# Sums of squares per token from ScalarE squares and column-tiled matmuls, in a two-block network on one core

## The chip, the core and the metric

The kernel runs on one core of a Trainium2 chip. A core has five engines with queues of their own: TensorE (PE, with a unit for loading weights, PEld), VectorE (DVE), ScalarE (ACT), GpSimd (POOL) and SyncE (SP, which here starts most transfers). Each takes its instructions in order, and semaphores hold an instruction until what it reads is written, or what it overwrites has been read. SBUF is the on-chip memory of 128 partitions; PSUM is where TensorE writes its sums, and ACT and DVE can read it. The metric is the device time of one execution, in microseconds.

## The reference

The reference is a network for 256 tokens of width 1024, in float32. A first block has a layer with a hybrid mixer and a dense feed-forward, and a layer with a Mamba-2 mixer and a mixture of eight experts. A second block has an even and an odd mixer, each with a squared-ReLU MLP, and works on the latent tokens and on a second set of 256 context tokens. In front of every mixer and feed-forward stands a normalization over the 1024 values of a token, followed by a modulation. The experts are chosen by router logits of the modulated tokens.

```python
def rmsnorm(x, w):
    y = xf * lax.rsqrt(jnp.mean(xf * xf, axis=-1, keepdims=True) + NORM_EPS)
    return y * w
def modulate(x, norm_w, shift, scale):
    return rmsnorm(x, norm_w) * (1 + scale) + shift
def moe_ffn(h, router, w_gu, w_down):
    logits = h @ router                        # 256 x 8
    top_val, top_idx = lax.top_k(logits, TOP_K)
    ...
# first block, the layer with experts
            mix = mamba2_mixer(modulate(x, ssm_norm[i], shift, scale), ...)
            x = x + gate * mix
            ffn = moe_ffn(modulate(x, moe_norm[i], shift, scale), ...)
            x = x + gate * ffn
```

So the sum of xf * xf over the 1024 values of each token is needed at each normalization.

## The kernel before

The activations are kept transposed: `x` is a tile of 128 partitions by 8 by 256, where the 1024 values of a token lie over 128 partitions and 8 slices k, and the 256 tokens are columns. `cx` is the same for the context. Weights are streamed from HBM by SP (`raw`, line 421), split by ACT into a rounded half `whi` and by DVE into the rest `wlo` (lines 426 and 429), and multiplied in three matmuls per pair (lines 446 to 448, 508 to 511, 565 to 567). Projections go to PSUM tiles `pws`, `praw`, `pm`; the output projection of a mixer or an MLP sums in `oacc` (lines 565 to 567), and then DVE adds it into `x` slice by slice (`resid`, line 891).

`square_sums` (line 598) gives the sum of squares of each token. Eight slices times two halves of the tokens make sixteen matmuls: a slice of 128 tokens is both the stationary and the moving operand, so that the 128x128 result in PSUM (`pss`) has the sums on its diagonal. DVE then multiplies each of two results with the identity and sums the rows (line 610), which gives one column of sums for each half. `rstd` scales on DVE (line 593) and takes the power -1/2 on POOL (line 595); `tok_rows` (line 631) multiplies the column by the identity on PE, which writes the factor of each token into every partition (`prb`). `norm_k` applies factor and modulation (lines 709 to 711: DVE, ACT, DVE).

There are twelve calls: at the start (`rms`, line 2553); in front of the dense feed-forward and of the Mamba mixer (`raw_mod`, line 681, where the projection runs on unnormalized data, `praw`, and the factor `rb` is applied to its result); in front of the experts (line 1564); two in the double normalization between the blocks (`two_norms`, lines 649 and 652); four for latent and context in the second block (`rms`, after each slice of the output projection has been added); one more `raw_mod` in front of the last MLP; and one at the end (line 2607).

In front of the experts the router's logits are sixteen matmuls (line 1571) with a slice of `x` as stationary operand and 8 columns of `AR` (router times modulation) as moving operand; DVE scales them by the factor of the token and adds the part of the shift (line 1574, `lg`). Ranks, lists of tokens per expert, the gathering matmuls (line 1672) and the experts' weights follow.

At the start the filters of the odd mixer are made while the first transfers run: a matmul `pfl` (line 2088), an eviction `fl` on DVE (line 2089), an absolute value on ACT (line 2091), summing matmuls `phn` with ones (line 2092), a reciprocal on DVE (line 2094), further products on DVE (lines 2101 to 2105), and the transform `pH` (line 2117). Between them PE computes the modulation `pada` (line 828): four matmuls of 128x32 by 512 columns, each into another group of 32 columns of the array.

The order of the instructions on each engine is not that of the code: a planner in the framework places each instruction where its operands are expected to be ready, so work of neighbouring steps stands between the parts of a function. `h_t` is a tag of two buffers in which `norm_k` and `square_sums` keep short-lived tiles.

## Time and profile before

| quantity | value |
| --- | --- |
| time, median of three | 2732.47 us (2728.77 to 2732.86) |
| the profiled execution | 2731.91 us, its span 2729.8 us |
| TensorE busy | 2612.9 us (96%) |
| VectorE busy | 1805.1 us (66%) |
| ScalarE busy | 1141.4 us (42%) |
| GpSimd busy | 74.1 us (3%) |
| granted clock of TensorE, mean | 0.986 of full speed |
| HBM traffic | 240 GB/s over the span |

The time of an execution is a little longer than the span, which runs from the first to the last instruction in the profile. Busy times of engines overlap. The ends of matmuls are modelled and matmuls are pipelined, so their lengths add up to more than the time that they hold PE; how long a group holds PE is read from the start of the next group. In the order of events, brackets give how long the engine sat idle before an instruction and whose end released it; a row with xN gathers N records without a break. A float32 matmul makes two records.

### The profile page before, as it was taken

To read this page: it belongs to the slowest core of one execution; us is meant where nothing else is said; L and a number is where in the kernel's file an instruction comes from. 1 tells how busy PE (TensorE), PEld (TensorE's weight loads), DVE (VectorE), ACT (ScalarE), POOL (GpSimd) and SP (SyncE) were. 2 spreads that over 40 slices of the span, in tenths; PEclk is the share of its full clock that TensorE was granted. 3 is DMA by queue.
4 is the path that set the end of the run, shared out by engine and by line. 5 is a ranking of instruction groups with operands and counts; after the bars stand their busy time and mean duration, and the time that the engine had idled before them with its cause. 6 is when DMAs were issued, how large, how long until landed. Compare 5 with 4: busy or idle time off the path is not lost. (4 is left out here: it accounts for less than half of the span.)

```text
span 2729.8 us, 42989 instructions
## 1 busy us (share of the span) xinstructions
PE 2612.9 (96%) x17432; PEld 2090.2 (77%) x17432; DVE 1805.1 (66%) x2970; ACT 1141.4 (42%) x1635; POOL 74.1 (3%) x117
## 2 busy tenths in 40 slices
PE   6999999999899999999999999989999999989999
PEld 2768999879755665566555589479889999879999
DVE  5485888887645655555545579678857548787754
ACT  3354445554644444444444432443223225313543
POOL 0100000000000000000000000000000001000000
PEclk9999999999899999999999999989999999999999
DMA  7655885543799999999999932334555303302552
GB/s 253 221 186 203 338 336 208 189 179 139 288 406 423 408 425 421 413 372 420 411 413 422 381 123 78 139 147 155 210 191 216 124 18 104 121 9 91 205 187 90
DMA packets 92780, 659.49 MB, mean 242 GB/s; under 512 B 10548, under 2 KB 10821, under 8 KB 13918
## 3 DMA queue, kind: packets, MB, share of 16 engines
q1 hardware_dynamic: 89582, 641.62, 60.1%
q0 software_dynamic: 2992, 15.04, 1.6%
q8 instruction: 139, 2.28, 0.3%
q14 instruction: 67, 0.55, 0.1%
HBM read 651.38 MB, written 4.72 MB: 240 GB/s over the span
## 5 line engine op out<-in xcount | busy, mean ns | idle before, releaser
L429 DVE TENSOR_TENSOR wlo<-wraw,whi 128x1024 fp32r<-128x1024 f32 (+1 forms) x683 | 811.3, 1217 | 337.9 <-ACT whi L426 334.3
L426 ACT ACTIVATE whi<-wraw 128x1024 fp32r<-128x1024 f32 (+1 forms) x683 | 705.2, 1054 | 719.1 <-PE oacc L566 182.0
L565 PE MATMUL oacc<-act_h,whi 128*128 128x256 f32 (+1 forms) x720 | 226.9, 316 | 0.0
L566 PE MATMUL oacc<-act_l,whi 128*128 128x256 f32 (+1 forms) x720 | 226.8, 315 | 0.0
L567 PE MATMUL oacc<-act_h,wlo 128*128 128x256 f32 (+1 forms) x720 | 226.8, 315 | 0.0
L794 DVE SCALAR_TENSOR_TENSOR macc<-wraw,srow 128x1024 f32<-128x1024 f32 x144 | 175.8, 1221 | 7.0 <-DMA wraw<-in_ada_dram 2.7
L567 PEld LDWEIGHTS oacc<-act_h,wlo 128*128 128x128 f32 x720 | 135.7, 188 | 10.1
L565 PEld LDWEIGHTS oacc<-act_h,whi 128*128 128x128 f32 x720 | 135.6, 189 | 10.0
L566 PEld LDWEIGHTS oacc<-act_l,whi 128*128 128x128 f32 x720 | 135.6, 188 | 10.0
L509 PE MATMUL pm<-h_lo,whi 128*128 128x256 f32 x512 | 132.8, 280 | 0.0
L508 PE MATMUL pm<-h_hi,whi 128*128 128x256 f32 x512 | 132.2, 277 | 0.0
L429 DVE TENSOR_TENSOR eal<-pat,eah 128x512 fp32r<-128x512 f32 x28 | 19.3, 691 | 167.0 <-ACT eah L426 167.0
L508 PE MATMUL pws<-h_hi,whi 128*128 128x256 f32 x416 | 112.1, 282 | 4.8 <-DVE xg L644 4.8
L1755 PE MATMUL pu<-wraw,gq 128*64 128x512 f32 x448 | 113.4, 595 | 0.0
L509 PE MATMUL pws<-h_lo,whi 128*128 128x256 f32 x416 | 111.4, 282 | 0.0
L1760 ACT ACTIVATE ea<-pg 128x512 f32<-128x512 f32 x42 | 25.1, 597 | 203.9 <-PE pg L1755 162.8
L447 PE MATMUL pyl<-wlo,eah 128*128 128x512 f32 x224 | 90.5, 404 | 18.6 <-DVE wlo L429 17.5
L511 PE MATMUL pm<-h_hi,wlo 128*128 128x256 f32 x512 | 106.9, 279 | 0.0
L446 PE MATMUL pws<-h_hi,whi 128*128 128x256 f32 x352 | 103.5, 294 | 0.0
L1761 DVE TENSOR_TENSOR ea<-ea,pu 128x512 f32<-128x512 f32 x42 | 28.9, 687 | 112.3 <-PE pu L1755 79.7
L1755 PE MATMUL pg<-wraw,gq 128*64 128x512 f32 x448 | 101.4, 596 | 0.0
L448 PE MATMUL pws<-h_hi,wlo 128*128 128x256 f32 x352 | 101.1, 287 | 0.0
(788 smaller groups left out, 6411.0 us busy)
## 6 DMA issues: line engine op xcount, KB each, us to landing
wraw<-in_moe_gu_dram SPq DMA_DIRECT2D x224, 1024.0 KB, 10.0
wraw<-in_moe_down_dram SPq DMA_DIRECT2D x112, 1024.0 KB, 9.7
wraw<-in_mlp_dram SPq DMA_DIRECT2D x64, 1024.0 KB, 4.8
wraw<-in_ada_dram SPq DMA_DIRECT2D x48, 1024.0 KB, 4.8
wraw<-in_dense_gu_dram SPq DMA_DIRECT2D x22, 1024.0 KB, 5.9
wraw<-in_hyb_mod_dram SPq DMA_DIRECT2D x12, 1024.0 KB, 6.8
wraw<-in_dense_mod_dram SPq DMA_DIRECT2D x12, 1024.0 KB, 4.8
wraw<-in_ssm_xbc_dram SPq DMA_DIRECT2D x12, 1024.0 KB, 4.8
```

Of the source, the lines that this page charges most:

```text
L426: self.nc.scalar.activation(hi, src, AF.Copy)
L429: self.nc.vector.tensor_tensor(lo, src, hi, op=OP.subtract)
L446: mm(out, l[0], r[0], start=start, stop=False)
L448: mm(out, l[1], r[0], start=False, stop=stop)
L508: mm(p[:, i], hi[:, k], hs[i][0][:, k], start=st, stop=False, skip_group_check=True)
L509: mm(p[:, i], hi[:, k], hs[i][1][:, k], start=False, stop=False, skip_group_check=True)
L511: mm(p[:, i], lo[:, k], hs[i][0][:, k], start=False, stop=k == 7, skip_group_check=True)
L565: mm(p, wh, h, start=start, stop=False, skip_group_check=True)
L566: mm(p, wh, l, start=False, stop=False, skip_group_check=True)
L567: mm(p, wl, h, start=False, stop=stop, skip_group_check=True)
L794: nc.vector.scalar_tensor_tensor(junk, r[:, j], 1.0, s, op0=OP.mult, op1=OP.mult, accum_out=t[:, f:f + 1])
L1755: mm(pg[gu][q], g[2][:, i, q], w[:, k], start=i == 0, stop=i == 7, skip_group_check=True)
```

## The change

`square_sums` is written anew. ACT squares two slices at a time into a tile of the tag `h_t` (128x512, four instructions). Eight matmuls with a stationary operand of ones, 128x32, run over 256 columns each and write 32 partitions of `pss`; slice k goes to column group k modulo 4, so that two slices are summed in each group. ACT copies the 128x256 result to SBUF, and two matmuls of one column with 1/32 as moving operand sum over the 128 partitions (each sum stands 32 times in its group), one for each half of the tokens. The result stays in PSUM, and line 593 reads it there. The sums of the router's logits are formed in the same way: `AR` is padded with zeros from 8 to 32 columns by a memset on POOL and is the stationary operand, ACT copies the four groups, and two matmuls with `four` (the sum of four pieces of the identity, from three adds on DVE) add them.

```diff
--- before.py
+++ after.py
@@ -359,6 +359,8 @@
         self.mhalf = self.cst.tile([128, 8], F32, name="mhalf")
         nc.gpsimd.memset(self.mhalf, -0.5)
         self.ident = self.k("ident")
+        self.one32 = self.cst.tile([128, 1], F32, name="one32")
+        nc.vector.memset(self.one32, 1.0 / 32)
 
     def c(self, name, i=0, n=None):
         o, w = self.at["cols"][name]
@@ -597,18 +599,22 @@
 
     def square_sums(self, x, ps=None):
 
+
         nc = self.nc
-        pss = (ps or self.ps)("pss", (128, 2, 128))
-        for k in range(8):
-            for tt in range(2):
-                c = slice(tt * 128, tt * 128 + 128)
-                nc.tensor.matmul(pss[:, tt], x[:, k, c], x[:, k, c], start=k == 0 and tt == 0, stop=k == 7,
-                                 skip_group_check=True)
-        ss = self.sm.tile([128, 2], F32, name="ss")
-        junk = self.hp.tile([128, 2, 128], F32, name="rj", tag="h_t", bufs=2)
+        pss = (ps or self.ps)("pss")
+        for k2 in range(4):
+            sq = self.hp.tile([128, 2, 256], F32, name="sqk", tag="h_t", bufs=2)
+            nc.scalar.activation(sq, x[:, 2 * k2:2 * k2 + 2], AF.Square)
+            for j in range(2):
+                k = k2 * 2 + j
+                q = slice(k % 4 * 32, k % 4 * 32 + 32)
+                nc.tensor.matmul(pss[q, :256], self.ones[:, :32], sq[:, j], start=k < 4, stop=k >= 4, skip_group_check=True)
+        part = self.hp.tile([128, 256], F32, name="sqp", tag="h_t", bufs=2)
+        nc.scalar.activation(part, pss[:, :256], AF.Copy)
+        ss = pss[:, 256:258]
         for tt in range(2):
-            nc.vector.scalar_tensor_tensor(junk[:, tt], pss[:, tt], 1.0, self.ident, op0=OP.mult, op1=OP.mult,
-                                           accum_out=ss[:, tt:tt + 1])
+            nc.tensor.matmul(ss[:, tt:tt + 1], part[:, tt * 128:(tt + 1) * 128], self.one32, start=True, stop=True,
+                             skip_group_check=True)
         return ss
 
     def col_sums(self, p, sq, start=True, stop=True):
@@ -1531,8 +1537,9 @@
 
     nc = S.nc
     R = S.c("router").rearrange("p (k e) -> p k e", e=8)
-    AR = S.cst.tile([128, 8, 8], F32, name="AR")
-    nc.vector.tensor_tensor(AR, R, S.mod(key, "A")[:, :, None].to_broadcast([128, 8, 8]), op=OP.mult)
+    AR = S.cst.tile([128, 8, 32], F32, name="AR")
+    nc.gpsimd.memset(AR, 0.0)
+    nc.vector.tensor_tensor(AR[:, :, :8], R, S.mod(key, "A")[:, :, None].to_broadcast([128, 8, 8]), op=OP.mult)
     p = S.ps("psr", (128, 8))
     s = S.mod(key, "S")
     for k in range(8):
@@ -1554,6 +1561,10 @@
         wk = st.enter_context(tc.tile_pool(reuse_waits="tile", name="moew", bufs=2))
         iota = mp.tile([128, 128], F32, name="iota")
         nc.gpsimd.iota(iota, pattern=[[1, 128]], base=0, channel_multiplier=0, allow_small_or_imprecise_dtypes=True)
+        four = mp.tile([128, 8], F32, name="four")
+        nc.vector.tensor_tensor(four, S.ident[:, 0:8], S.ident[:, 32:40], op=OP.add)
+        for q in (64, 96):
+            nc.vector.tensor_tensor(four, four, S.ident[:, q:q + 8], op=OP.add)
         st.enter_context(S.extra(raw=4, big=2))
         xr = S.rings["r"][2]
         ohp = st.enter_context(tc.tile_pool(reuse_waits="tile", name="moeh", bufs=1))
@@ -1565,10 +1576,15 @@
         r = mp.tile([128, 2], F32, name="rtok")
         nc.vector.tensor_copy(r, S.rstd(ss, 1024))
 
-        pl = S.ps("plog", (128, 2, 8))
+        pq = S.ps("plog", (128, 512))
+        for k in range(8):
+            q = slice(k % 4 * 32, k % 4 * 32 + 32)
+            mm(pq[q, :256], AR[:, k], x[:, k], start=k < 4, stop=k >= 4, skip_group_check=True)
+        lq = wk.tile([128, 256], F32, name="lq", tag="ea")
+        nc.scalar.activation(lq, pq[:, :256], AF.Copy)
+        pl = pq[:, 256:272].rearrange("p (t e) -> p t e", t=2)
         for tt in range(2):
-            for k in range(8):
-                mm(pl[:, tt], x[:, k, tt * 128:(tt + 1) * 128], AR[:, k], start=k == 0, stop=k == 7)
+            mm(pl[:, tt], lq[:, tt * 128:(tt + 1) * 128], four, start=True, stop=True, skip_group_check=True)
         lg = mp.tile([128, 2, 8], F32, name="lg")
         for tt in range(2):
             nc.vector.scalar_tensor_tensor(lg[:, tt], pl[:, tt], r[:, tt:tt + 1], SR, op0=OP.mult, op1=OP.add)
```

The planner gives other orders. The first place is DVE's queue at the start, up to the second reciprocal `finv`, and the rows begin two instructions behind the first reciprocal in before and just behind it in after. An `fl` from `pfl` is an eviction of the filter; lines 2089, 2094 and 2101 to 2105 of before are 2105, 2110 and 2117 to 2121 of after.

```order
L2103 TENSOR_TENSOR fl<-g_372,finv 128x512
L2104 TENSOR_TENSOR fl<-fl,finv 128x512
L2101 SCALAR_TENSOR_TENSOR g_377<-fl,k_hy 128x512
L2105 TENSOR_TENSOR fl<-fl,hskip 1x512
L2102 TENSOR_TENSOR fl<-fl 128x512
L2089 TENSOR_TENSOR fl<-pfl,k_hy_93 128x512 x2
L2103 TENSOR_TENSOR fl<-g_377,finv 128x512
L2104 TENSOR_TENSOR fl<-fl,finv 128x512
L2089 TENSOR_TENSOR fl<-pfl,k_hy_93 128x512
L2101 SCALAR_TENSOR_TENSOR g_383<-fl,k_hy 128x512
L2102 TENSOR_TENSOR fl<-fl 128x512
L2094 RECIPROCAL finv<-phn 128x512
```

And in the changed kernel:

```order
L2105 TENSOR_TENSOR fl<-pfl,k_hy_95 128x512 x2
L2119 TENSOR_TENSOR fl<-g_374,finv 128x512
L2120 TENSOR_TENSOR fl<-fl,finv 128x512
L2105 TENSOR_TENSOR fl<-pfl,k_hy_95 128x512
L2117 SCALAR_TENSOR_TENSOR g_379<-fl,k_hy 128x512
L2121 TENSOR_TENSOR fl<-fl,hskip 1x512
L2118 TENSOR_TENSOR fl<-fl 128x512
L2119 TENSOR_TENSOR fl<-g_379,finv 128x512
L2110 RECIPROCAL finv<-phn 128x512
```

Between the two reciprocals stand four evictions in before (the first of them is the row right behind the first reciprocal, not shown) and three in the changed kernel, because ahead of the first reciprocal stand five of them instead of four. Three products (2104, 2101 and 2102 in the lines of before) have moved from the front of the second reciprocal to behind it.

The second place is ACT's queue after the first MLP's context part (near 1866 us): `whi` is the split of a weight slice, `h_hi` the modulation, whose `Sc` is that of the context and `Sl` that of the latent tokens.

```order
L426 ACTIVATE whi<-wraw 128x1024
L710 ACTIVATE h_hi<-h_t,mod_01Sc 128x256 x2
L426 ACTIVATE whi<-wraw 128x1024
L710 ACTIVATE h_hi<-h_t,mod_01Sl 128x256 x8
L426 ACTIVATE whi<-wraw 128x1024
```

And in the changed kernel:

```order
L716 ACTIVATE h_hi<-h_t,mod_01Sc 128x256 x2
L428 ACTIVATE whi<-wraw 128x1024
L716 ACTIVATE h_hi<-h_t,mod_01Sc 128x256
L607 ACTIVATE sqk<-x 128x512 x4
L613 ACTIVATE sqp<-pss 128x256
L716 ACTIVATE h_hi<-h_t,mod_01Sl 128x256 x8
```

The four squares and the copy of the sums stand between the last weight split and the modulation of the latent tokens, behind that split.

The third place is PE's queue at the context call near 2219 us, inside the output projection of the latent tokens (`oacc`).

```order
L566 MATMUL oacc<-act_l,whi 128x256
L567 MATMUL oacc<-act_h,wlo 128x256
L605 MATMUL pss<-cx 128x128 x16
L565 MATMUL oacc<-act_h,whi 128x256
L566 MATMUL oacc<-act_l,whi 128x256
L567 MATMUL oacc<-act_h,wlo 128x256
```

And in the changed kernel:

```order
L569 MATMUL oacc<-act_h,wlo 128x256
L611 MATMUL pss<-sqk,ones 32x256 x4
L567 MATMUL oacc<-act_h,whi 128x256
L568 MATMUL oacc<-act_l,whi 128x256
L569 MATMUL oacc<-act_h,wlo 128x256
L567 MATMUL oacc<-act_h,whi 128x256
L568 MATMUL oacc<-act_l,whi 128x256
L569 MATMUL oacc<-act_h,wlo 128x256
L611 MATMUL pss<-sqk,ones 32x256 x2
L567 MATMUL oacc<-act_h,whi 128x256
L611 MATMUL pss<-sqk,ones 32x256 x2
L568 MATMUL oacc<-act_l,whi 128x256
```

The sixteen matmuls in one piece are replaced by eight tile matmuls in three pieces, with output matmuls between them.

## Rows read from the trace of the kernel before

**Rows 1.** The page: the span, and busy time of each engine.

```profile
span 2729.8 us, 42989 instructions
...
PE 2612.9 (96%) x17432; PEld 2090.2 (77%) x17432; DVE 1805.1 (66%) x2970; ACT 1141.4 (42%) x1635; POOL 74.1 (3%) x117
```

**Rows 2.** Stretches: window, length, busy PE, PEld, DVE, ACT, POOL, clock, DMA, GB/s.

```profile
75.00:246.00 171.00, 168.46 (x1117) 130.51 (x1116) 98.66 (x233) 72.25 (x156) 13.81 (x22) 1.00 0.56 203
697.00:1578.00 881.00, 848.17 (x3756) 522.31 (x3756) 476.81 (x509) 416.64 (x470) 0.00 (x0) 0.99 0.97 403
```

**Rows 3.** Line 605, the sums' matmuls: ns min/median/max, first and last start.

```profile
L605 PE MATMUL pss<-x x288: 270/275/579, 23.5 to 2722.3; 128*128 128x128 f32 x144
```

**Rows 4.** Order of events, 37 to 41: start, length, engine, operation.

```profile
37.85 1.13 PE L2092 MATMUL phn<-fab,ones 128*128 128x512 f32 x2
...
38.91 1.06 PE L828 MATMUL pada<-wraw,cblk 128*32 128x512 f32 x8
...
39.90 1.13 PE L2092 MATMUL phn<-fab,ones 128*128 128x512 f32 x2
```

**Rows 5.** Lines 1457 and 681, ACT's Square and a copy: ns min/median/max.

```profile
L1457 ACT ACTIVATE zsq<-y x8: 614/628/634, 526.8 to 641.9; 128x512 f32<-128x512 f32 x8
...
L681 ACT ACTIVATE rb<-prb x3: 383/385/386, 260.9 to 2541.5; 128x256 f32<-128x256 f32 x3
```

**Rows 6.** Order of events at the start, 23 to 80; brackets: idle before, releaser.

```profile
23.49 4.80 PE L605 MATMUL pss<-x 128*128 128x128 f32 x32
...
41.06 3.36 DVE L2094 RECIPROCAL finv<-phn 128x512 f32<-128x512 f32 x1 [2.42 <-PE phn L2092]
...
45.68 1.12 PE L2092 MATMUL phn<-fab,ones 128*128 128x512 f32 x2 [1.75 <-ACT fab L2091]
...
54.77 3.36 DVE L2094 RECIPROCAL finv<-phn 128x512 f32<-128x512 f32 x1 [1.82 <-PE phn L2092]
...
69.46 1.50 PE L2117 MATMUL pH<-fl,k_hy 128*128 128x512 f32 x2 [3.83 <-DVE fl L2105]
...
79.44 0.68 PE L448 MATMUL psm<-h_hi,wlo 128*64 128x256 f32 x1
```

**Rows 7.** Order of events at 1866.

```profile
1866.49 3.73 PE L605 MATMUL pss<-x 128*128 128x128 f32 x32
1866.63 1.06 ACT L426 ACTIVATE whi<-wraw 128x1024 fp32r<-128x1024 f32 x1 [1.03 <-PE oacc L566]
...
1870.81 0.17 DVE L593 TENSOR_SCALAR rstdv<-ss 128x2 f32<-128x2 f32 x1
...
1871.81 0.71 PE L631 MATMUL prb<-kb,rstd 128*128 128x128 f32 x4 [1.58 <-POOL rstd L595]
```

**Rows 8.** PE by stretches: window, length, busy, clock, DMA share, GB/s.

```profile
258.00:260.00 2.00, 1.04 (x4) 0.50 0.04 8
262.00:264.00 2.00, 2.00 (x11) 0.50 0.54 225
```

**Rows 9.** Order of events at the router, 680 to 698.

```profile
680.03 3.73 PE L605 MATMUL pss<-x 128*128 128x128 f32 x32
...
683.60 3.64 PE L1571 MATMUL plog<-AR,x 128*128 128x8 f32 x32
...
685.36 0.17 DVE L1566 COPY rtok<-rstd 128x2 f32<-128x2 f32 x1 [0.84 <-POOL rstd L595]
...
687.28 0.36 DVE L1574 SCALAR_TENSOR_TENSOR lg<-plog,rtok,SR 128x8 f32<-128x8 f32 x2 [1.75 <-PE plog L1571]
...
697.17 0.97 SPq L421 DMA_DIRECT2D wraw<-in_moe_gu_dram  x2
```

**Rows 10.** Order of events, 1855: a broadcast.

```profile
1855.51 0.71 PE L631 MATMUL prb<-kb,rstd 128*128 128x128 f32 x4 [0.54 <-POOL rstd L595]
```

**Rows 11.** Order of events at 2235 and 2534.

```profile
2235.72 1.06 ACT L426 ACTIVATE whi<-wraw 128x1024 fp32r<-128x1024 f32 x1 [0.87 <-PE oacc L566]
...
2534.12 3.25 DVE L679 SCALAR_TENSOR_TENSOR h_lo<-x,mod_11Al,h_hi 128x256 fp32r<-128x256 f32 x8
```

## The prediction

> **What bounds the kernel now.** I read the page's first lines, then the busy time by stretches, then the line of the changed function, and last the order of events at each of its twelve calls. TensorE (PE) is busy 2612.9 of 2729.8 us [rows 1]. Between the calls it is the bound with transfers to spare (75 to 246 us: PE 168.46 of 171.00, DMA share 0.56); only in the experts' stretch, 697 to 1578 us, are the DMA engines full, at 0.97 [rows 2]. So time that PE gains at a call is kept up to the next call, and what the router gains is kept if the experts' transfers start earlier with it. The change must be priced call by call: how much PE work goes, and whether PE then waits for ScalarE (ACT).
>
> **Prices.** Sixteen full-array matmuls of 128 columns make 32 records of 0.275 us, which overlap [rows 3]: before the router they start at 680.03 and the next matmul at 683.60, so a call holds PE 3.6 us. The router's own 32 records hold it 3.64 us [rows 9]. Four tile matmuls of 512 columns, one in each column group, already run in this kernel: they start at 38.91, and the next full-array matmul starts at 39.90, as a full-array matmul of 512 columns before them held PE from 37.85 to 38.91 [rows 4]. So four tiles run side by side in the time of one, and a block of 256 columns costs half of 1.06, 0.53 us. A block of two tiles, cut off by other work, I price like one of four, since each tile's columns are as many. A matmul of one column I take at two records of the router's spacing, 3.64/32 x 2 = 0.23 us; two per call are 0.45. The Square of 128x512 has an exact counterpart, 0.628 us, and the copy of 128x256 out of PSUM too, 0.385 us [rows 5]: four and one are 2.9 us of ACT per call, where ACT is 42% busy [rows 1]. VectorE loses two diagonal extractions with their accumulator reads, which counts only where the rstd chain is waited for. The moe's memset and three small adds run on engines that are idle there; I cost them nothing, and 0.5 us if they are not.
>
> The Trainium skill (TensorEngine Tiling (Array Packing), Key Properties) says that changing the tiling mode drains TensorE, and the change puts some 40 blocks of tiles between full-array matmuls. The rows of 37.85 to 39.90 show no price for it: 1.06 us from the matmul before the tiles to the tiles, 0.99 from the tiles to the matmul behind [rows 4]. By the rule the sum is too good by whatever a drain takes, by the rows it stands; the drain is the fourth rival below.
>
> **The sum, call by call.** From the order of the changed kernel I count into how many blocks the eight tile matmuls of a call are cut. A call with b blocks frees 3.6 - 0.53 b - 0.45 us of PE; then I ask what is late next.
> - Start, 23 to 80 us (all eight in a row, two blocks): 4.80 - 1.06 - 0.45 = 3.3 us of work [rows 6]. The order changes too. Before, a reciprocal of 3.36 us stands in VectorE's queue ahead of filter steps on which PE then waits, 1.75 us at 45.68 and 3.83 us at 69.46. Now one more eviction stands ahead of the first reciprocal, and the second comes three instructions earlier. The work ahead of the first one's fourth summing matmul falls by the 3.3 us, and one filter matmul has changed places with one block of the modulation's: from 41.06 to about 38. The second, at 54.77, gains these 3, the wait of 1.75, and three instructions of 0.7: about 48. So PE's two waits go. At most 3.3 + 1.75 + 3.83 = 8.9 us; at least 2, if new waits take their place. I take 7, near the upper end, because both waits sit on instructions that move ahead, and keep 1.9 for waits on the squares and on POOL.
> - 246 us (three blocks): 1.5 of work; the tail runs at half clock already [rows 8], and the broadcast waits for POOL; 1.0 (0 to 3).
> - 446 us (three): 1.5 of work, but the residuals on VectorE then bound; 0.9 (-1 to 2).
> - Router, 680 us (four, and three for the logits): 7.2 - 7 x 0.53 - 0.9 = 2.6 of work. The logits are combined at 687.28 after a wait for PE, and need rstd as well, copied at 685.36 for 0.17 [rows 9]. So at most 1.75 goes, and I take 1.7. The experts' first transfers, issued at 697.17, come as much earlier.
> - 1582 us (two calls, seven blocks): 7.2 - 3.7 - 0.9 = 2.6. The row broadcast comes about 2 us later in the work, but projections fill that; 2.5 (0 to 4).
> - 1850 and 2219 us (three blocks each, with output matmuls between them): 1.6 each of work, and the wait for rstd (0.54 at 1855.51 [rows 10]) goes under cover, but the residuals come later; 1.4 each (0 to 2).
> - 1866 us: here nothing is left to stand between. All eight tiles stand in a row, then copy, sums, rstd, broadcast. ACT's queue has a weight split ahead of the squares that waits for PE until 1866.63 and takes 1.06 [rows 7]. From 1867.7 four squares end near 1870.2, the last tiles 1870.5, the copy 1870.9, the two sums 1871.35; rstd and the broadcast start 1.0 later, as before (1870.81 to 1871.81), and five handovers of about 0.1 make it 1872.9 instead of 1871.81: a loss of about 1.2. PE does one microsecond of work in 6.5. Where its busy time was as low as 1.04 of 2 us, at 258, the granted clock read 0.50, which is the 1.2 GHz level, and it still did at 262 to 264 with PE busy throughout [rows 8]. One such stretch costs up to 3 us; I take 1.5 (0 to 3). Together -2.7.
> - 2235 us (four blocks, after eight projection matmuls): 1.0 of work, but the split at 2235.72 is ahead of the squares again [rows 11], and PE waits about 1.3 for the first and 0.4 for the second; -0.7 (-3 to 1).
> - 2533 us (three): the 1.5 of work is lost, because the projection waits for residuals that VectorE begins at 2534.12 and needs 3.25 us for [rows 11], and the broadcast is later; -0.3 (-2 to 1).
> - The last call: transposes hide the work, and the chain to the output is as long as before; 0.
>
> Sum: 7 + 1.0 + 0.9 + 1.7 + 2.5 + 1.4 + 1.4 - 2.7 - 0.7 - 0.3 = 12.2 us. The profiled execution took 2731.91 us, 2.1 of them around its span, and 0.56 less than the median of 2732.47. So 2731.91 - 12.2 = 2719.7, or 2720.3 by the median: 2720.
>
> **Rivals.**
> 1. PE's removed work counts in full. 12 x 3.6 + 3.6 = 46.8 us go, 40 blocks x 0.53 + 26 x 0.23 = 27.2 come: 19.6 net, and 2 us of the start's waits: 2710. For it: PE at 96%. Against it: at 1866 and 2533 us the squares or the residuals stand in the way.
> 2. The gain is hidden: the start keeps 2 us, because its waits move to another filter step, and the other gains (8.9 together) are halved by what is late next, while the three losses of 3.7 stay: 2731.9 - 2 - 4.5 + 3.7 = 2729. For it: both reciprocals of 3.36 us remain on the chain. Against it: PE's waits there stand plainly in the rows, and between the calls it hardly waits.
> 3. Slower: ACT stands in PE's way. PE takes its queue in order, so a tile matmul ahead of its square holds up all that follows. If ACT's splits come first, as at 1866 us, at the nine calls other than the start, that one and the last, each loses 1.2 instead of its gain, and half of them 1.5 for the clock. At five of nine: 5 x 1.2 + 2.5 x 1.5 + 2.7 = 12.5 against the start's 7 and 4 x 1.3 kept: no change. From there it is slower; at seven 16.4 against 9.6, 2739, and at nine 2746. I take 2739. For it: the rows of 1866 and 2235 us. Against it: elsewhere the order leaves several matmuls between two blocks.
> 4. Tiles cost more than their rows: each of 80 changes from or to tiles takes another 0.275 us, one record [rows 3], 22 us in all against the 12.2: 2742. The rule of the Trainium skill named above would act in this way. Against it: rows 4.
>
> **How the numbers follow.** The forecast has 0.50 (its own range 2714 to 2726, from the bounds at the start and at 1866 us), the full count 0.12, the hidden gain 0.21, the waits for ACT 0.13, the switches 0.04. This kernel's measurement can tell 0.2%, 5.5 us, from no change. Faster by more: nearly all of the forecast (0.48), the full count and a third of the hidden gain (0.07): 0.67. Slower by more: nearly all of the waits and of the switches and no more than a trifle else, 0.14 at most. Between: 0.19. The range 2710 to 2735 leaves out half of the full count and most of the two slower cases.
>
> **What would show it.** Eight tile matmuls in a row in 1.1 us, not 2 or more; squares of 0.63 us; the reciprocals near 38 and 48 and no wait for a filter step before 72 us; the experts' first transfer 7 + 1 + 0.9 + 1.7 = 10.6 us earlier than 697; at 1866 us a broadcast 6.5 us after the last output matmul, and a granted clock near 0.5 behind it. The forecast is wrong if PE's waits before tile matmuls, released by ACT, sum to over 8 us, or if the start's gain stays under 4.

## The result: 0.6% slower, and the profile after

The changed kernel took 2749.13 us (median; 2748.42 to 2753.39), the kernel before in the same session 2732.66: ratio 1.0063, interval 1.0051 to 1.0075. It is slower by 16.5 us where 12 us of gain were forecast. The page of the changed kernel, the lines that answer to [rows 1]:

```profile
span 2746.6 us, 42751 instructions
...
PE 2621.9 (95%) x17276; PEld 2074.1 (76%) x17276; DVE 1801.6 (66%) x2926; ACT 1171.8 (43%) x1696; POOL 74.6 (3%) x118
```

There are 156 matmul records fewer (78 matmuls, two records each), yet PE is busy 9.0 us longer. If each removed matmul freed time, this should have fallen, so the first thing to look for is something that makes other matmuls slower. I paired equal matmuls of the two traces in order, and took the median difference of their starts per 20 us of before. The changed kernel's start earlier by 9.0 at 80 us and 4.6 at 100, level at 410, later by 5.4 at 480, 5.8 at 700, 5.1 at 1600, 9.1 at 1900, 12.1 at 2240, and 16.0 at 2680. So there are jumps, at calls, and a steady loss between them, where no instruction was changed.

The prices of the forecast were right where no square is waited for. Order of events of the changed kernel in front of the Mamba mixer (start, length, engine, line; x8 and x4 count two records a matmul): four tile matmuls and the full-array matmul behind them, and a block of two and what stands behind it:

```profile
450.15 0.64 PE L611 MATMUL pss<-sqk,ones 128*32 128x256 f32 x8
450.72 0.51 PE L448 MATMUL praw<-h_hi,whi 128*128 128x258 f32 x2
...
454.53 0.63 PE L611 MATMUL pss<-sqk,ones 128*32 128x256 f32 x4
455.09 0.39 PE L449 MATMUL praw<-h_lo,whi 128*128 128x258 f32 x1
```

The starts are 0.57 and 0.56 us apart, where 0.53 was taken for either. The squares and copies took the 0.63 and 0.38 that their counterparts took [rows 5]. By the rule of the Trainium skill that a change of the tiling mode drains TensorE (TensorEngine Tiling (Array Packing), Key Properties) these blocks should hold PE longer; with both switches in them they exceed the price by 0.04 us, so the trace has no drain of a size that matters.

And what ended PE's and the weight loads' idle time before these matmuls (line 611, the profile's view of one line):

```profile
L611 PE MATMUL pss<-sqk,ones x192: 379/379/636, 22.9 to 2738.2; 128*32 128x256 f32 x192
...
its engine sat idle before it (us, times) until:
  ACT sqk L607: 14.3, 19
```

The 14.3 us add up PE (4.1 in five waits, the longest 1.95 at 1875 us) and its weight loads (10.2), which run ahead of it. The 4.1 are too few, because the modelled lengths cover gaps. At the first call the eight tile matmuls follow the squares:

```profile
24.29 1.15 PE L611 MATMUL pss<-sqk,ones 128*32 128x256 f32 x8 [0.77 <-ACT sqk L607]
```

They held PE from 22.88 to 25.37, 2.5 us, and 2.7 at 1875, where the prediction had 1.1 "and not 2 or more": four squares of 0.63 take that long. Taking 0.56 us for each block from what it holds PE, and adding the idle time, I estimate some 8 us of waits in all, 1.4 of them at the start and 3.5 at 1866. That is on the edge of the 8 that the prediction named as a refutation. But from 12.2 us of gain to the 11.5 of loss that the calls turned out to cost (below) it is 23.7, so a direct wait for the squares is not the main part.

### The profile page after: what moved, and what is told of

It reads as the page before. It is cut to its first block, busy times and chain, and to the rows that moved or that the text cites. A ratio compares the mean times of both kernels' runs of the same rounds, so it can differ in the third digit from the quotient of the medians.

```text
span 2746.6 us, 42751 instructions
## 1 busy us (share of the span) xinstructions
PE 2621.9 (95%) x17276; PEld 2074.1 (76%) x17276; DVE 1801.6 (66%) x2926; ACT 1171.8 (43%) x1696; POOL 74.6 (3%) x118
## 5 line engine op out<-in xcount | busy, mean ns | idle before, releaser
L568 PEld LDWEIGHTS oacc<-act_l,whi 128*128 128x128 f32 x720 | 136.5, 190 | 10.2 <-issue 0.4
L511 PE MATMUL pws<-h_lo,whi 128*128 128x256 f32 x416 | 112.8, 285 | 0.0
L449 PE MATMUL pws<-h_lo,whi 128*128 128x256 f32 x352 | 101.8, 289 | 0.0
```

Of the source, the lines that this page charges most:

```text
L449: mm(out, l[0], r[1], start=False, stop=False)
L511: mm(p[:, i], hi[:, k], hs[i][1][:, k], start=False, stop=False, skip_group_check=True)
L568: mm(p, wh, l, start=False, stop=False, skip_group_check=True)
```

## The experiments

All times are medians, and each ratio is against runs of the kernel before on the same chip (2732.0 to 2733.4).

**Which part, and is it the place of the data?** First guess: the change puts a 4-byte tile `one32` (32 bytes with padding) in front of the others and a 32-byte tile `four` into the router, so all that follows lies 32 bytes further. `pad` is the changed kernel with both padded to 64 bytes; `shift32` is the kernel before with the 4-byte tile. `sums_pad` has the new sums with the old logits, `router_only` the new logits with the old sums.

```diff
 pad:     -        self.one32 = self.cst.tile([128, 1], F32, name="one32")
          +        self.one32 = self.cst.tile([128, 16], F32, name="one32")
 shift32: +        self.one32 = self.cst.tile([128, 1], F32, name="one32")
          +        nc.vector.memset(self.one32, 1.0 / 32)
```

> The changed kernel with its two new small constants (one32, four) made 64 bytes long per partition instead of 4 and 32; every engine's instructions stand in the same order. In the changed kernel the constant of 4 bytes takes 32 bytes of SBUF and moves nearly every later tile (x, the split weights, the modulated activations) from an address that is a multiple of 64 to one that is 32 beyond it; here they are back on multiples of 64. Theory A (the addresses): between the calls of square_sums the matmuls of the changed kernel follow each other 0.120 us apart instead of 0.117, some 14 to 17 us over the span, and that goes away: 2749 becomes 2732 to 2736, with the spacing back at 0.117. Theory B (the calls themselves: PE waits 14.3 us for squares and the chains end later): the time stays at 2749 within 3 us, and the spacing is not what it depends on.

> The kernel before with only the constant one32 of 4 bytes added at the same place (one memset on VectorE, never read), so that the later tiles move by 32 bytes; the sums and the router are those of before. Theory A (addresses): 2745 to 2750, and the matmuls between the calls 0.120 us apart. Theory B (calls): 2732.5 within 3 us.

> The new square_sums with the padded constant, and the router of before; addresses on multiples of 64. Theory A: the calls on their own change little, since what they free of PE is lost in waits for the squares and in the weights' arrival at the start: 2732 to 2738. Theory B: 2749 to 2752, because it keeps all waits for squares and loses the router's 1.7.

> The new router logits (with the constant four padded to 64 bytes) and the square_sums of before. Both theories: the router gives the 1.7 us of the forecast, 2729 to 2732; if its padded operand or the transfers of the experts take that back, 2732.5 to 2735.

Measured: pad 2756.67 (ratio 1.0078, 1.0064 to 1.0091), shift32 2735.29 (1.0002, .9993 to 1.0011), sums_pad 2753.53 (1.0084, 1.0068 to 1.0099), router_only 2731.04 (.9990, .9981 to .9998). So 32 bytes cost less than 0.12%, the guess fell, and the new logits by themselves gain a little. The whole loss is with the sums.

**The place, second try.** Where the trace has neither a call nor a wait, between 290 and 440 us, PE is busy throughout at granted clock 1.00. The windows' columns are those of [rows 2]; the number of matmuls behind PE's busy time is what to read. The kernel before:

```profile
290.00:440.00 150.00, 150.00 (x1283) 150.00 (x1282) 127.19 (x186) 66.48 (x90) 0.00 (x0) 1.00 0.89 333
```

The changed kernel:

```profile
290.00:440.00 150.00, 150.00 (x1253) 150.00 (x1252) 124.68 (x180) 65.67 (x88) 0.00 (x0) 1.00 0.84 322
```

And pad:

```profile
290.00:440.00 150.00, 150.00 (x1252) 150.00 (x1252) 126.62 (x181) 66.15 (x87) 0.00 (x0) 1.00 0.86 328
```

1283 matmuls in 150 us have become 1253: each takes 0.1197 us instead of 0.1169, with the same instructions. In the kernel before, two spacings stand in one line (446 to 448), the projection `pgu`, for two buffers of weights (its order of events on PE, by the starts):

```profile
293.05 0.28 PE L447 MATMUL pgu<-h_lo,whi 128*128 128x256 f32 x1
293.16 0.28 PE L448 MATMUL pgu<-h_hi,wlo 128*128 128x256 f32 x1
293.28 0.28 PE L446 MATMUL pgu<-h_hi,whi 128*128 128x256 f32 x1
...
297.10 0.28 PE L446 MATMUL pgu<-h_hi,whi 128*128 128x256 f32 x1
297.22 0.28 PE L447 MATMUL pgu<-h_lo,whi 128*128 128x256 f32 x1
297.34 0.28 PE L448 MATMUL pgu<-h_hi,wlo 128*128 128x256 f32 x1
```

0.113 and 0.120 us. I took the addresses of all tiles from the compiled program and sorted the spacings of neighbouring 256-column matmuls by the address of the moving operand less that of the next matmul's stationary operand, which is loaded meanwhile, modulo 128 bytes. Before: 119.7 ns at 0 (1524 pairs), 116.0 ns at 64 (1006 pairs). After: 119.9 ns at 0 (2462 pairs), and nearly none at 64. What moved them is a removal: the old sums' result `ss` was a tile of two 32-byte buffers in the pool `sm`, and now the sums stay in PSUM. The pools behind `sm` thus lie 64 bytes nearer to those ahead of it. In the program the pairs at 64 fall from 5637 to 1829.

`relayout` is pad with those two buffers allocated again, unused; `sm64` is the kernel before with 64 unused bytes in `sm`; `best` has unused tiles that put most pairs at 64 (11243), and `after_best` the same on top of relayout.

```diff
 relayout: +        self.sm.tile([128, 2], F32, name="ss")
 sm64:     +        self.sm.tile([128, 8], F32, name="fill")
 best:     +        self.fa.tile([128, 16], F32, name="filla")
           +        self.sm.tile([128, 8], F32, name="fill")
           ... and a tile of 64 bytes ahead of the extra h pools
```

> The changed kernel with its small constants padded to 64 bytes as in pad, and with the two 32-byte buffers that the old square_sums had for its sums (ss, in the pool of small tiles) still set aside, though nothing uses them; same instructions in the same order. Theory A fell in the form that it had (a shift of all tiles by 32 bytes cost 2 us at most). New form, theory A2 (relative addresses): in the trace of before, matmuls whose moving operand and whose successor's weights start a multiple of 128 bytes apart follow each other after 119.7 ns, those that start 64 more apart after 116.0 ns; the removed 64 bytes lie between the pool of the activations and the pools behind it, and turn some 3000 pairs outside the experts' stretch from the second kind into the first: 3000 x 3.9 ns = 12 us. Then 2749 becomes 2736 to 2739. Theory B (the calls alone, squares waited for): 2749 to 2757, as pad.

> The kernel before with 64 bytes more in the pool of small tiles (an unused tile of 8 columns, two buffers), which flips the same relation as the change did; no instruction differs. A2: 2900 pairs more at multiples of 128 bytes, 2733 + 11.4 = 2743 to 2747. B: 2733 within 2 us.

> The kernel before with three fillers of 64 bytes (ahead of the activations' pool, in the pool of small tiles, ahead of the additional weight halves), chosen so that weights and moving operand start 64 bytes apart modulo 128 nearly everywhere outside the experts' stretch; no instruction differs. A2: about 4500 pairs leave the slow kind, 4500 x 3.9 ns = 17 us: 2713 to 2719. B: 2733 within 2 us.

> relayout with the fillers of best. A2: 2737 - 17 = 2720, 2717 to 2723. B: 2749 to 2757.

Measured: relayout 2743.83 (1.0042, 1.0028 to 1.0055), sm64 2744.03 (1.0037, 1.0023 to 1.0052), best 2729.41 (.9988, .9978 to .9998), after_best 2736.55 (1.0012, 1.0001 to 1.0024). The same window in relayout:

```profile
290.00:440.00 150.00, 150.00 (x1283) 150.00 (x1282) 127.68 (x184) 66.66 (x89) 0.00 (x0) 1.00 0.86 329
```

In sm64:

```profile
290.00:440.00 150.00, 150.00 (x1262) 150.00 (x1261) 126.48 (x184) 64.57 (x86) 0.00 (x0) 1.00 0.87 327
```

And in best:

```profile
290.00:440.00 150.00, 150.00 (x1276) 150.00 (x1275) 127.60 (x184) 64.74 (x86) 0.00 (x0) 1.00 0.88 333
```

sm64 decides it: not one instruction differs, 64 unused bytes cost 10 us, and the window loses 21 matmuls. relayout has the instructions of pad, and the window is back at 1283. So the layout costs 5.7 us (the changed kernel less relayout) to 9.8 (pad less relayout), either uncertain by 5, and the calls themselves the rest, 11.5. best moved the right way, but 3 us where 13 to 19 were expected, and after_best gained 7.3 on relayout where some 20 were expected. In the window best has even fewer matmuls than the kernel before, 1276 against 1283, with nearly all pairs at 64: the spacing at 64 differed between kernels (116.0 to 117.6). So the difference modulo 128 is not the whole rule, and I cannot say which finer property of the addresses decides. SBUF — State Buffer of the Trainium skill says, in its section on the wrong intuition of a bandwidth pool, that TensorE has a second, independent read port for loading weights. By that alone one would not expect the place of one operand to matter for the other; the 21 to 30 matmuls of the window say that it does, whatever the cause. That the two reads collide is a guess, only the relation is shown.

**Which call loses?** relayout with the old sums back at two places (446 and 1866 us) is `undo_cg`; `only_de` has the new sums at the router and in the double normalization and the new logits; `start_only` has the new sums at the first call alone; `best2` is best with wider unused tiles. Calls are numbered in the order of the program; 4 is the router's, 5 and 6 are the double normalization's.

```diff
 in square_sums, ahead of the new code (square_sums_full is the old one):
 undo_cg:    +        self.nss = getattr(self, "nss", 0) + 1
             +        if self.nss not in (1, 2, 4, 5, 6, 7, 9, 10, 11, 12):
             +            return self.square_sums_full(x, ps)
 only_de:    the same with (4, 5, 6); start_only with (1,), and the old logits
 best2:      -        self.fa.tile([128, 16], F32, name="filla")
             -        self.sm.tile([128, 8], F32, name="fill")
             +        self.fa.tile([128, 48], F32, name="filla")
             +        self.sm.tile([128, 24], F32, name="fill")
             +        self.cst.tile([128, 16], F32, name="fillc")
```

> relayout with the old square_sums at two calls, in front of the Mamba mixer (446 us) and at the latent call near 1866 us; the other ten calls are new. Place theory: between the traces of before and relayout the distance of the same matmuls grows by 3.4 us across the first place and by some 4 across the second (of which 5.1 us at the 1.2 GHz level between 1872 and 1884 us take half), so relayout's 2743.8 falls by 7 to 2735 to 2738. Spread theory (each block of tiles costs PE a little wherever it stands): a sixth of the loss of 11 goes, 2741 to 2743.

> The new square_sums only at three calls, in front of the experts and in the double normalization, and the new router logits; old at the other nine; small tiles laid out as in before. Place theory: these places gain 1.9 and 2.3 us in relayout's trace: 2732.4 - 4.2 = 2728 (2726 to 2730). Spread theory: 3 of 12 calls lose 3 us and the router gives 2: 2733.

> The new square_sums only at the first call; old at the eleven others, and the old router. The forecast gave this place -7 (2725.5). From relayout's trace: 8.4 us are gained by 82 us, 1.6 of them are lost at a wait for the transfer of a weight block near 98 us, and 4.4 more because TensorE then runs at 1.2 GHz from 100 to 112 us; 2 remain: 2730 (2729 to 2733).

> The kernel before with fillers that put the moving operands at multiples of 256 bytes and the weights 64 beyond them, where the traces so far show 113.5 ns per matmul (before: 119.8, 117.6 and 113.9, by group); best stood at 117.6 nearly everywhere. Address theory: some 7000 matmuls of 256 columns outside the experts' stretch gain 4 ns on average, 28 us, as far as TensorE stays the bound: 2705 to 2715. If transfers, ScalarE or VectorE take over as the bound, as the small gain of best (3 us of an expected 12) may mean: 2722 to 2729.

Measured: undo_cg 2736.64 (1.0019, 1.0007 to 1.0032), only_de 2735.97 (1.0012, 1.0002 to 1.0021), start_only 2730.13 (.9992, .9981 to 1.0002), best2 2728.93 (.9984, .9972 to .9997). Two of twelve calls make up 6.3 of the 11.5 us that the calls cost, where 7 were expected; the difference is uncertain by 5. only_de missed: 2736 where 2728 was expected. Its trace is 2.0 us ahead of that of before in front of the router and 3.3 behind that call, but 1.8 late at the double normalization, so it lost in the experts' stretch. Four more runs part that pair and put the gaining pieces together: `only_e` (double normalization alone), `only_d` (router's call and new logits), `combo` (best2 with calls 1, 5, 6) and `combo_r` (combo with the new logits).

```diff
 only_e:  +        if self.nss not in (5, 6):    (old logits)
 only_d:  +        if self.nss not in (4,):      (new logits)
 combo:   +        if self.nss not in (1, 5, 6): (old logits) and the tiles of best2
 combo_r: as combo, with the new logits
```

> The new sums at the two calls of two_norms alone; start, dense feed-forward, Mamba, router and second block have the old sums, the router's logits are the old ones, and the layout of the pools is that of before. The prediction's term for this place is 2.5 us, and the traces with the new sums everywhere showed 2.3 here. If a gain on the path in the place stays, 2730 (ratio .9991). If the mixers behind it, which wait for transfers, give it back, 2732 to 2733 (1.0000). If the new sums themselves cost time on the way (as the pair of this place and the router's did, 2736 where 2728 was expected), 2735 and more.

> The new sums at the call in front of the experts and the new logits of the router, the old sums elsewhere, the layout of before. The new logits alone measured .999 of the kernel before. If places add up, another 1 us for the sums: 2729 (.9987). If the stretch of the experts, whose weights arrive at their own pace, gives the gain back, 2731 to 2733. If the miss of the pair (2736) comes from this call, 2735 to 2737 here, while the kernel with the new sums at the two other calls alone stays at or under 2732.

> The kernel before with the filling tiles of best2 (which alone measured .9984 of the kernel before, 2728.9), and the new sums at the start and in two_norms alone. If the places and the layout add up: 2728.9 less .5 to 2 at the start and less 2 at two_norms, 2725 to 2727 (.9975). If two_norms' gain is given back, 2728 to 2729; if calls cost on the way, 2731 and more.

> As the combination before it, and the new logits of the router (old sums there), which alone measured .999 of the kernel before. If all adds up, 2723 to 2725 (.9965), the fastest of all. If the experts' stretch gives the router's gain back when the layout speeds up PE in it, as the one before it (2725 to 2727). If the combinations lose what the parts showed, 2729 and more, no better than the filling tiles alone.

Measured: only_e 2732.90 (.9998, .9989 to 1.0007), only_d 2736.99 (1.0013, 1.0004 to 1.0022), combo 2725.77 (.9971, .9959 to .9983), combo_r 2720.26 (.9957, .9943 to .9971). only_d names the culprit, the sums in front of the router: the kernels router_only and only_d differ in them and in a constant of 64 bytes, which only_e and start_only have without a loss. What they do is seen at the experts' first weights, in the order of events. ACT of router_only:

```profile
701.13 1.06 ACT L426 ACTIVATE whi<-wraw 128x1024 fp32r<-128x1024 f32 x1
```

Its PE:

```profile
702.25 0.80 PE L446 MATMUL pg<-whi,gh 128*128 128x512 f32 x1 [2.27 <-ACT whi L426]
```

ACT of only_d:

```profile
700.83 0.56 ACT L1735 ACTIVATE h_t<-pgat,mod_moeSl,mod_moeAl 128x256 f32<-128x256 f32 x1 [1.09 <-PE pws L1724]
...
703.25 2.00 ACT L428 ACTIVATE whi<-wraw 128x1024 fp32r<-128x1024 f32 x2
```

And its PE:

```profile
704.36 0.79 PE L448 MATMUL pg<-whi,gh 128*128 128x512 f32 x1 [3.62 <-ACT whi L428]
```

The gathering starts 0.8 us later in only_d (692.77 against 691.94); then ACT's queue stands in another order, with one more split of gathered tokens (`gh`) ahead of the first weight split and the wait of 1.09 us for PE, and that split comes 2.1 us later, and with it PE's first projection. 2.9 us are left at 1558 in these two executions, of 6 in the medians.

The products of the parts' ratios are .9974 for combo and .9964 for combo_r, the measurements .9971 and .9957: the pieces add up, and combo_r beats both kernels, by 12 us and by 29. Its page:

```profile
span 2718.1 us, 42916 instructions
...
PE 2602.9 (96%) x17384; PEld 2074.7 (76%) x17384; DVE 1804.3 (66%) x2962; ACT 1149.6 (42%) x1651; POOL 74.6 (3%) x118
```

## Why the prediction was wrong, step by step

By the ratios, each uncertain by 2 to 5 us, 1 us being 0.00037:

| piece | forecast | measured | from |
| --- | --- | --- | --- |
| layout of the pools | not in the sum | -5.7 | after, relayout |
| start | +7 | +2.2 | start_only |
| 446 and 1866 us | +0.9, -2.7 | -6.3 | relayout, undo_cg |
| router: logits, sums | +1.7 in all | +2.7, -6.3 | router_only, only_d |
| double normalization | +2.5 | +0.5 | only_e |
| the other calls | +2.8 | about -4 | what is left of 11.5 |

**A term was missing.** "The change must be priced call by call" left out what a removed tile does to all other matmuls. The sign for it stood in the trace of before: two spacings, 0.113 and 0.120 us, in one line at 293 and 297 us.

**The start: right about its place, wrong about what is kept.** Both reciprocals came about a microsecond before the forecast, PE's waits of [rows 6] at 45.68 and 69.46 went, and the projection `pws` began at 73.38 instead of 82.34; 1.5 of these 9.0 us come from a first transfer that landed earlier in this execution (PE's first matmul at 11.81, not 13.28), so the forecast of 7 was met there. The reciprocals in VectorE's order of events in the changed kernel:

```profile
36.90 3.36 DVE L2110 RECIPROCAL finv<-phn 128x512 f32<-128x512 f32 x1 [0.37 <-PE phn L2108]
46.87 3.36 DVE L2110 RECIPROCAL finv<-phn 128x512 f32<-128x512 f32 x1 [0.70 <-PE phn L2108]
```

Then the gain is given back. ACT's order of events before:

```profile
105.10 2.01 ACT L426 ACTIVATE whi<-wraw 128x1024 fp32r<-128x1024 f32 x2 [3.85 <-DMA wraw<-in_hyb_qk_dram]
```

And in the changed kernel:

```profile
98.17 2.00 ACT L428 ACTIVATE whi<-wraw 128x1024 fp32r<-128x1024 f32 x2 [5.88 <-DMA wraw<-in_hyb_qk_dram]
```

And a window of the kernel before (columns as in [rows 2]):

```profile
108.00:112.00 4.00, 4.00 (x27) 3.16 (x26) 2.01 (x7) 0.00 (x0) 0.56 (x1) 1.00 1.00 420
```

Three of the changed kernel:

```profile
98.00:101.00 3.00, 0.26 (x1) 0.27 (x2) 2.62 (x4) 2.58 (x4) 0.59 (x1) 0.89 0.50 142
101.00:106.00 5.00, 5.00 (x20) 3.94 (x20) 1.83 (x6) 0.00 (x0) 0.56 (x1) 0.50 0.96 385
106.00:111.00 5.00, 5.00 (x23) 4.49 (x23) 4.36 (x9) 0.00 (x0) 0.54 (x1) 0.54 0.48 174
```

The next weights, `in_hyb_qk`, are issued 6.9 us earlier than before (93.36, not 100.30) but wanted earlier still: ACT waits 5.88 us for them (3.85 before), PE is busy 0.26 of 3 us, and the granted clock reads 0.50 and 0.54 for the next ten, the 1.2 GHz level, with PE busy throughout, where it read 1.00 before. The prediction's claim that PE "is the bound with transfers to spare", from a mean DMA share of 0.56 [rows 2], did not hold for one transfer. start_only keeps 2.2 of it (between -0.5 and 5.2), under the 4 that the prediction named as its own refutation, if not by a clear margin.

And in some executions the start gains nothing to begin with. Nine of the profiled kernels have the new sums there. In six of them the second reciprocal comes at 46.8 to 48.4 us; in pad, undo_cg and combo it comes at 54.8 to 55.6, as late as before (54.77), because PE ran the filters' matmuls at half the pace. A window of the changed kernel:

```profile
28.00:32.00 4.00, 3.97 (x17) 1.65 (x18) 2.65 (x4) 1.26 (x2) 0.00 (x0) 1.00 0.80 301
```

And of undo_cg:

```profile
28.00:32.00 4.00, 4.00 (x8) 1.65 (x7) 0.16 (x1) 0.11 (x1) 0.71 (x1) 1.00 0.85 354
```

PE is busy in both and the granted clock reads 1.00 in both, but 17 records have become 8. None of the nine profiled kernels with the old sums at the start shows this. In the six traces read for this, PE begins the transposes ahead of the first call at the lower pace, records of 128 columns 0.21 us apart. Before, the distance falls to 0.11 at 25.6 us, inside the 32 records of the old sums; in the changed kernel and relayout it does so near the end of the transposes (21.8 and 22.8), and in the three it had not, and the pace rose only near 41. So the old sums may have bridged what the new ones, with their waits for squares, leave open. That is argued, not tested. So the start's share of a median may be a mixture, in pad too, where it can be part of the 9.8 us; sm64 has the old sums and is free of it.

**446 us: -1 to 2 was too narrow.** The prediction asked for PE's work and for waits before tiles. What lost was the chain to the factor `rb`. The order of events in the changed kernel, on ACT and, in the fifth row, on PE:

```profile
448.76 3.28 ACT L684 ACTIVATE h_hi<-x,mod_ssmAl 128x256 fp32r<-128x256 f32 x8
451.95 1.14 ACT L607 ACTIVATE sqk<-x 128x512 f32<-128x512 f32 x2
453.10 1.28 ACT L1492 ACT_TABLE_LOAD   x1
...
456.14 0.39 ACT L613 ACTIVATE sqp<-pss 128x256 f32<-128x256 f32 x1 [1.51 <-PE pss L611]
...
457.74 0.50 PE L616 MATMUL pss<-one,sqp 128*128 128x1 f32 x4
...
460.20 0.38 ACT L687 ACTIVATE rb<-prb 128x256 f32<-128x256 f32 x1 [2.80 <-PE prb L637]
```

And in the kernel before, where ACT had nothing to do with the sums:

```profile
453.31 0.29 DVE L610 SCALAR_TENSOR_TENSOR rj<-pss,kb 128x128 f32<-128x128 f32 x1 [0.26 <-PE pss L605]
...
455.78 0.39 ACT L681 ACTIVATE rb<-prb 128x256 f32<-128x256 f32 x1 [4.62 <-PE prb L631]
```

`rb` comes 4.4 us later, though the residuals in front of the call begin only 0.6 later (446.42, not 445.80). The last two squares stand in ACT's queue behind the eight `h_hi` (3.28 us) and end at 453.09, about when the old sums were ready. The loss is in what follows: the tile matmuls have their turn in PE's queue at 454.53 and 455.41, the copy comes at 456.14, and the one-column matmuls have theirs at 457.74, each time with projection matmuls ahead of them. The table load behind the squares does not delay the copy, since ACT is idle 1.51 us after it. PE has projections to do meanwhile, as forecast, so its busy time shows nothing yet. VectorE, which needs `rb`, shows it, in two windows of the kernel before:

```profile
452.00:458.00 6.00, 6.00 (x54) 6.00 (x53) 3.72 (x17) 1.82 (x5) 0.69 (x1) 1.00 0.01 3
...
470.00:476.00 6.00, 6.00 (x43) 4.85 (x42) 6.00 (x12) 2.44 (x5) 0.10 (x1) 1.00 0.52 183
```

And of the changed kernel:

```profile
452.00:458.00 6.00, 6.00 (x49) 4.75 (x45) 2.15 (x9) 3.40 (x7) 0.00 (x0) 1.00 0.51 178
...
470.00:476.00 6.00, 3.33 (x20) 1.57 (x20) 6.00 (x13) 3.26 (x5) 0.21 (x2) 0.98 0.47 149
```

VectorE works 2.15 of 6 us where it worked 3.72. Later it is busy all 6.00, as before, but PE now gets only 3.33 beside it: what VectorE lost in waiting is lacking 20 us on, where PE waits for it:

```profile
474.44 0.31 PE L1487 MATMUL pdtt<-kb,dT 32*128 32x32 f32 x2 [1.85 <-DVE dT L1484]
```

relayout shows the same stretch (PE 3.32).

**1866 us: the mechanism right, the size too small.** The order of events of the changed kernel on ACT:

```profile
1873.48 1.06 ACT L428 ACTIVATE whi<-wraw 128x1024 fp32r<-128x1024 f32 x1 [1.02 <-PE oacc L568]
1874.84 2.68 ACT L607 ACTIVATE sqk<-x 128x512 f32<-128x512 f32 x4
...
1878.30 0.38 ACT L613 ACTIVATE sqp<-pss 128x256 f32<-128x256 f32 x1 [0.79 <-PE pss L611]
```

And on PE:

```profile
1875.50 2.69 PE L611 MATMUL pss<-sqk,ones 128*32 128x256 f32 x16 [1.95 <-ACT sqk L607]
...
1880.44 0.71 PE L637 MATMUL prb<-kb,rstd 128*128 128x128 f32 x4 [1.10 <-POOL rstd L597]
```

As forecast, the split stands ahead of the squares and waits for PE. But the squares begin 1.56 us after the last output matmul (1873.28), not 1.2, the split's end being followed by one more `h_hi`, and the copies and sums behind them are later too: from that matmul to the broadcast are 7.2 us, not 6.5. The half clock behind it, for which 1.5 us were taken from a bound of 3, is there in relayout, absent in this execution of the changed kernel (1.00). Two windows of relayout:

```profile
1872.00:1878.00 6.00, 4.33 (x20) 1.57 (x20) 2.00 (x4) 2.23 (x4) 0.70 (x1) 0.57 0.51 173
1878.00:1884.00 6.00, 5.99 (x31) 5.99 (x32) 4.36 (x11) 2.33 (x6) 0.00 (x0) 0.57 0.00 1
```

0.57 over 12 us is 5 us, beyond the bound.

**Router and double normalization: right in the trace, not in the time.** The forecast gains of 1.7 and 2.5 are there as 1.9 and 2.8 between the matmuls of before and relayout in front of and behind these places, but the router's is gone by the experts' matmuls at 712 us. Of them the medians kept 2.7 less 6.3 and 0.5, and only_e's own trace has 0.6 for the double normalization. At the router, with the sums changed too, ACT's queue stands in an order that delays the experts' weights; "kept if the experts' transfers start earlier" was not enough. The first transfer of the experts, forecast 10.6 us earlier than 697.17 [rows 9], came at 701.64 in the changed kernel. In router_only it came at 692.31, with 2.6 of these 4.9 us gained before the router.

**The rivals.** The full count and the hidden gain fell. The tile switches fell by the pairs above. The waits for ACT came nearest: 2739, or 2746 with nine calls, against 2743.83 for the calls alone (relayout). But their mechanism was only half right: ACT does stand in the way of the tile matmuls (some 8 us), but the larger part lies elsewhere, as far as it was found: in the chain from the sums to the factor and to whoever needs it, and in the experts' weights. Its chance of 0.13 was too low, since ACT was treated as an engine that is 42% busy, not as a queue with something ahead of the squares at every call.

What stays open: what the "other calls" lost one by one, which was not tried (at 2235 the forecast waits of 1.3 and 0.4 did not come, each block held PE 0.56); 3 of the 6 us of the router's call; what sets the pace of the start; and the finer rule of the addresses.

## What to carry to other kernels

Work that moves from a matrix engine to an engine on the chain behind it is priced by the queues at each place: what stands ahead of each link of the new chain, on either engine, and which engine idles for the result, not the one that gave up work. Any edit that adds or removes a tile also moves the others: put an unused tile of the same size in its stead, time that too, and only then judge the edit. A change that gains at some places and loses at others should be split, since the gaining places alone, with a chosen layout, were worth 12 us.

## What the runs showed of the hardware

The spacing of 256-column matmuls at full clock depends on where operands lie: 0.113 to 0.120 us in one line of one kernel, 119.7 to 119.9 ns where the moving operand and the next stationary one lie a multiple of 128 bytes apart, 116.0 ns at 64 bytes off in the kernel before. 64 unused bytes changed a kernel by 0.37% (sm64). A move of everything by 32 bytes changed the time by less than 0.12% (shift32).

A block of two or of four tile matmuls (32 columns of the array each, 256 columns moved) between full-array matmuls held PE 0.56 to 0.57 us, both switches included (450 and 454 us of the changed kernel).

At the start PE ran at half pace up to some 41 us in three of nine profiled executions with the new sums there, with PE busy and the granted clock at 1.00 (17 records against 8 in 4 us).
